# Decay rows of two chunked scans: from a select matmul to a masked fill and an accumulating DMA

## The chip, the cores and the metric

The kernel runs on one core of a Trainium2 chip. The metric is the device time of one execution in microseconds (us); lower is better.

## What is computed

The reference is one step of a two-layer diffusion backbone over 640 tokens (128 of context, 512 of a latent grid) with a model width of 1024. Each layer has a normalised and modulated input, one wide input projection, three bidirectional recurrent mixers side by side (an SSD scan with 16 heads in 4 groups, an HGRN2 scan with 4 heads, an mLSTM scan with 4 heads), gated merging, an output projection, and a gated feed-forward block. Only the decay matrices of two of the scans matter here. In the SSD scan, with `la` the cumulative log decay inside a chunk:

```python
la = jnp.cumsum(dtc * a[:, None], axis=-1)
diff = jnp.where(causal, la[..., :, None] - la[..., None, :], 0.0)
seg = jnp.exp(diff) * causal * dtc[..., None, :]
```

The mLSTM scan has the same form: an exponential of a term of the row (time) plus a term of the column (source), zero where the mask forbids. The backward direction has the opposite triangle.

## The kernel before

The tokens are cut into five chunks of 128 (`NCH`), the first of which is the context. Activations are kept transposed, with features on the 128 partitions. Weights arrive as 512 KB tiles on the SyncE DMA queue (`weight_load`, called `wr` in the trace; three buffers), are split by ScalarE and VectorE into a rounded part and a remainder (`wh`, `wl`; four buffers each), and each tile of a projection is three matmuls of 320 columns per half and per block of 128 rows (`project`, `accumulate`, line 495).

TensorE's order is written out by hand: `drive` runs a scan as a generator and, at every `yield n`, runs n steps of the projections that still wait ("bulk"; one step is six matmuls of 320 columns). So a scan's own matmuls are strewn among projection matmuls. The order on ScalarE, VectorE, SyncE and GpSimd is chosen at build time by a planner, which goes by the order of the program and by when it takes operands and buffers to be free; at run time each queue is strictly in order. GpSimd does nothing but issue DMAs (`load`, line 138); SyncE issues those of `stream` (line 141). Most intermediate tiles come from one pool of 35 buffers of 128x656 (`ut`).

How the decay matrices come about, for one scan and one direction d:

- `store_rows` (line 798) transposes the cumulative decays of all heads and chunks into rows, splits each into a rounded part `rwh` and a remainder `rwl`, sets the remainder at the edge position to -1e30, and stores both in DRAM (`rows_s`, `rows_m`).
- `new_rows` (line 945) makes `NROW` = 2 buffers `rb` for each direction, filled by ScalarE with the additive mask (0 or -1e30), four copies side by side.
- `fetch_rows` (line 954) overwrites two partitions of such a buffer, those at the edge of the triangle, with the two parts of the rows, by a DMA of 2 to 4 KB on GpSimd's queue.
- `row_bank` (line 961) is the matmul that does both jobs: its stationary operand `rsel` is an identity in which the two partitions of the rows have ones in every column. The product in PSUM is the mask plus the row, on all 128 partitions.
- ScalarE takes the exponential from PSUM, with the column's term as its bias, into a tile `E` (SSD, line 1175; four heads of one chunk, four instructions of 128x128) or `mA` (mLSTM, line 1452; one head, chunk by chunk).

```python
rows = [row_bank(d, flats[c][d], 4) for d in range(2)]
fetch(c + NROW)
for d, pt in enumerate(rows):
    e = ut("E")
```

In `ssd_scan`, `stage_a(c)` holds these lines; `stage_b(c)` (the matmuls `py` that use `E`) comes two chunks later (`LAGB`), and the first two fetches are made at the first of the four state updates (after the copy `cx`). In `mlstm_scan` the rows of a head are fetched at its start, and are used after the four state updates, in two groups of three and two chunks. There are 4 SSD scans and 4 mLSTM scans per layer, 8 and 8 in the program.

## Time and profile before

| | |
|---|---|
| median of 3 runs | 2811.21 us (2811.20 to 2813.16) |
| the profiled execution, its own time | 2809.44 us |
| its span, first to last instruction | 2807.7 us |
| TensorE busy in the span | 2765.0 us (98%) |
| share of TensorE in the chain that ended last | 94% |
| matmuls of `row_bank` (line 963) | 112 |
| moved by DMA | 347.97 MB, 16 engines 37.4% busy on average |

The profile lists each engine's busy time, the waits with what ended them, and a timeline. A busy TensorE here is one that always has a next matmul at hand; consecutive matmuls overlap, so what one costs is the distance from its start to the start of the next, not its duration.

### The profile page before, as it was taken

The numbers are of one execution on the slowest core, as the hardware profiler recorded it, in microseconds if no ns is written. First come the engines' busy times: TensorE is split into PE (matmuls) and PEld (weight loads), VectorE is DVE, ScalarE is ACT, GpSimd is POOL, SyncE is SP. The second block draws the span as 40 slices with busy tenths as digits, with TensorE's granted clock in tenths as the row PEclk, the third lists the DMA queues.
The fourth block names the chain that finished last, engine by engine and source line by source line (L and its number), as shares of the span: only waits on it lengthen the run. The fifth ranks groups of instructions, "written<-read, shape, count | busy, mean of one in ns | idle before, by whom it ended". The sixth has DMA issues, their size and how long they took to land.

```text
span 2807.7 us, 48854 instructions
## 1 busy us (share of the span) xinstructions
PE 2765.0 (98%) x19374; PEld 2714.7 (97%) x19374; DVE 1902.0 (68%) x3862; ACT 1227.6 (44%) x2453; POOL 265.0 (9%) x499
## 2 busy tenths in 40 slices
PE   7999999999999999999999999999999999999998
PEld 6999999999999999999999999999999999999998
DVE  6566668777655586867776665878775556747475
ACT  5534434445542363343455444344455225425243
POOL 0111100001031100000001111000111201000000
PEclk9999999999999999999999999999999999999999
DMA  8222223333374314344522222333333732333433
GB/s 322 90 93 80 89 85 111 128 117 117 125 256 148 108 63 155 126 132 156 175 98 86 83 91 94 106 114 128 121 112 119 258 106 96 100 128 103 130 108 100
DMA packets 102579, 347.97 MB, mean 124 GB/s; under 512 B 18784, under 2 KB 22080, under 8 KB 102224
## 3 DMA queue, kind: packets, MB, share of 16 engines
q1 hardware_dynamic: 70704, 243.34, 26.2%
q0 software_dynamic: 31648, 101.52, 10.7%
q8 instruction: 153, 2.51, 0.4%
q14 instruction: 74, 0.61, 0.1%
HBM read 290.37 MB, written 54.42 MB: 123 GB/s over the span
## 4 chain that ended last, share of the span: by engine, by line
PE 94%; DVE 3%; ACT 2%; DMA 1%; issue 1%; SPq 0%; ACTq 0%; DVEq 0%
PE ga L423 17%; PE ab L495 15%; PE bg L495 12%; PE br L495 8%; PE sz L495 4%; PE hfp L495 4%; PE xT L495 4%; PE hl L1328 2%; PE ga L495 2%; PE hgp L495 2%; PE hqp L495 2%; PE mkp L495 2%; PE BT L495 2%; PE CT L495 2%; PE mop L495 1%; PE mqp L495 1%
## 5 line engine op out<-in xcount | busy, mean ns | idle before, releaser
L412 ACT ACTIVATE wh<-wr 128x1024 fp32r<-128x1024 f32 (+3 forms) x354 | 352.7, 1000 | 545.1 <-PE br L495 144.3
L413 DVE TENSOR_TENSOR wl<-wr,wh 128x1024 fp32r<-128x1024 f32 (+3 forms) x354 | 406.1, 1148 | 198.8 <-ACT wh L412 194.6
L423 PE MATMUL ga<-hb,wh 128*128 128x320 f32 x912 | 201.4, 308 | 0.0
L1588 DVE SCALAR_TENSOR_TENSOR x<-ab,hg,x 128x128 f32<-128x128 f32 (+2 forms) x192 | 73.2, 433 | 170.1 <-PE ab L495 170.1
L423 PE MATMUL ga<-hth,wl 128*128 128x320 f32 x608 | 187.7, 309 | 0.0
L423 PE MATMUL ga<-htl,wh 128*128 128x320 f32 x608 | 187.4, 308 | 0.0
L423 PE MATMUL ga<-hth,wh 128*128 128x320 f32 x608 | 187.4, 308 | 0.0
L495 PE MATMUL bg<-hh,wh 128*128 128x320 f32 x768 | 186.5, 324 | 0.0
L495 PE MATMUL bg<-hl,wh 128*128 128x320 f32 x768 | 174.8, 309 | 0.0
L495 PE MATMUL bg<-hh,wl 128*128 128x320 f32 x768 | 174.6, 308 | 0.0
L495 PE MATMUL ab<-uh,wh 128*128 128x320 f32 x704 | 164.5, 309 | 0.0
L495 PE MATMUL ab<-ul,wh 128*128 128x320 f32 x704 | 164.1, 309 | 0.0
L495 PE MATMUL ab<-uh,wl 128*128 128x320 f32 x704 | 164.0, 308 | 0.0
L423 PEld LDWEIGHTS ga<-hb,wh 128*128 128x128 f32 x912 | 152.4, 188 | 0.0
L423 PE MATMUL ga<-hb,wl 128*128 128x320 f32 x456 | 140.7, 308 | 0.0
L495 PEld LDWEIGHTS bg<-hh,wh 128*128 128x128 f32 x768 | 126.5, 189 | 2.4 <-issue 0.8
L495 PEld LDWEIGHTS bg<-hl,wh 128*128 128x128 f32 x768 | 128.4, 188 | 0.0
L495 PEld LDWEIGHTS bg<-hh,wl 128*128 128x128 f32 x768 | 128.4, 188 | 0.0
L495 PEld LDWEIGHTS ab<-ul,wh 128*128 128x128 f32 x704 | 118.8, 188 | 0.2
L495 PEld LDWEIGHTS ab<-uh,wh 128*128 128x128 f32 x704 | 118.6, 188 | 0.2
L495 PEld LDWEIGHTS ab<-uh,wl 128*128 128x128 f32 x704 | 118.7, 188 | 0.0
L423 PEld LDWEIGHTS ga<-hth,wh 128*128 128x128 f32 x608 | 114.3, 188 | 0.0
(505 smaller groups left out, 7542.0 us busy)
## 6 DMA issues: line engine op xcount, KB each, us to landing
wr<-w_in SPq DMA_DIRECT2D x152, 512.0 KB, 3.4
wr<-w_gu SPq DMA_DIRECT2D x88, 512.0 KB, 3.8
wa<-w_ada SPq DMA_DIRECT2D x84, 512.0 KB, 3.6
x<-xd POOLq DMA_DIRECT2D x64, 320.0 KB, 3.6
wr<-w_down SPq DMA_DIRECT2D x32, 512.0 KB, 3.8
sp<-bgt POOLq DMA_DIRECT2D x48, 320.0 KB, 3.4
bgr<-sp POOLq DMA_DIRECT2D x48, 320.0 KB, 4.8
xd<-x POOLq DMA_DIRECT2D x40, 320.0 KB, 2.5
```

The lines of the kernel that those rows point to most:

```text
L412: act.activation(out=hi[:, :n], in_=raw[:, :n], func=AF.Copy)
L413: dve.tensor_tensor(out=lo[:, :n], in0=raw[:, :n], in1=hi[:, :n].bitcast(F32), op=ALU.subtract)
L423: pe.matmul(bank_[:, :HALF], a_[:, sl], b_, start=first and j == m == 0, stop=j == n - 1 and m == 2, skip_group_check=True,)
L495: pe.matmul(out[hf][:, :HALF], wt_[:, sl], b_, start=m == k == 0, stop=m == 2 and k == n - 1)
L1328: pe.matmul(pt[:, (c - c0) * P : (c - c0 + 1) * P], kk[:, sl], halves_of(QK[:, 0, sl], 3 * T, L, P // (2 * L)), start=True, stop=True,)
L1588: dve.scalar_tensor_tensor(out=x_[:, lo:hi], in0=pt[:, lo - hf * HALF : hi - hf * HALF], scalar=gate[:, 2 * f + j : 2 * f + j + 1], in1=x_ ...
```

## The change

The matmul, its stationary operand and its mask buffers are removed. The rows are stored once, in full float32. For each `E` or `mA` tile a DMA on SyncE's queue first copies the mask into it (128 partitions, four or five times the same 128 floats), and then a DMA on GpSimd's queue adds the rows to it, read from DRAM for every partition anew. The exponential runs in place, from SBUF. An SSD scan fetches as many chunks ahead as before, but into `E` itself; an mLSTM scan fills both whole `mA` tiles at its start.

```diff
-        rows_s = dr.tile([4, NCH, SH, P], F32R, name=nm("rows_s"), tag="rows_s")
-        rows_m = dr.tile([2, 2, NCH, MH, P], F32R, name=nm("rows_m"), tag="rows_m")
+        rows_s = dr.tile([2, NCH, SH, P], F32, name=nm("rows_s"), tag="rows_s")
+        rows_m = dr.tile([2, NCH, MH, P], F32, name=nm("rows_m"), tag="rows_m")
...
-        def store_rows(src, n, d, dst_of):
+        def store_rows(src, n, d, dst):
             pt = bank("rows")
             pe.transpose(pt[:n, :P], src, ident)
-            hi = ut("rwh", F32R)
-            lo = ut("rwl", F32R)
-            act.activation(out=hi[:n, :P], in_=pt[:n, :P], func=AF.Copy)
-            dve.tensor_tensor(out=lo[:n, :P], in0=pt[:n, :P], in1=hi[:n, :P].bitcast(F32), op=ALU.subtract)
-            act.activation(out=lo[:n, EDGE[d] : EDGE[d] + 1], in_=cc[:n, C_MASKF, 0:1], func=AF.Copy, scale=0.0, bias=NEG)
-            load(dst_of(0), hi[:n, :P])
-            load(dst_of(1), lo[:n, :P])
+            row = ut("rw")
+            act.activation(out=row[:n, :P], in_=pt[:n, :P], func=AF.Copy)
+            act.activation(out=row[:n, EDGE[d] : EDGE[d] + 1], in_=cc[:n, C_MASKF, 0:1], func=AF.Copy, scale=0.0, bias=NEG)
+            load(dst, row[:n, :P])
...
-        def new_rows():
...
-        def fetch_rows(d, src, n):
...
-        def row_bank(d, flat, n):
-            pt = bank("row")
-            pe.matmul(pt[:, : n * P], rsel[:, d, :], flat[:, : n * P], start=True, stop=True)
-            return pt
+        def masked_rows(d, out, src, n):
+            v = out.rearrange("p (n t) -> p n t", t=P)
+            stream(v, cc[:, C_MASKF + d, :].unsqueeze(1).to_broadcast([P, n, P]))
+            nc.gpsimd.dma_start(out=v, in_=src.unsqueeze(0).to_broadcast([P, n, P]), accum_op=ALU.add)
+            return out
...
-                    flats[c] = [fetch_rows(d, rows_s[2 * d : 2 * d + 2, c, hsl, :], 4) for d in range(2)]
+                    flats[c] = [masked_rows(d, ut("E")[:, :512], rows_s[d, c, hsl, :], 4) for d in range(2)]
...
-                    if g == 0:
-                        new_rows()
...
-                E = []
-                rows = [row_bank(d, flats[c][d], 4) for d in range(2)]
+                E = flats.pop(c)
                 fetch(c + NROW)
-                for d, pt in enumerate(rows):
-                    e = ut("E")
+                for d, e in enumerate(E):
                     for j in range(4):
                         act.activation(
-                            out=e[:, j * P : (j + 1) * P], in_=pt[:, j * P : (j + 1) * P], func=AF.Exp,
+                            out=e[:, j * P : (j + 1) * P], in_=e[:, j * P : (j + 1) * P], func=AF.Exp,
...
-            if hd == 0:
-                new_rows()
-            flats = [[fetch_rows(d, rows_m[:, d, c0:c1, hd, :], c1 - c0) for d in range(2)] for c0, c1 in groups]
+            A = [masked_rows(d, ut("mA")[:, :T], rows_m[d, :, hd, :], NCH) for d in range(2)]
...
-            A = [ut("mA") for _ in range(2)]
...
-                    pt = row_bank(d, flats[c0 > 0][d], n)
                     for c in range(c0, c1):
                         sl = slice(c * P, (c + 1) * P)
-                        act.activation(out=A[d][:, sl], in_=pt[:, (c - c0) * P : (c - c0 + 1) * P], func=AF.Exp, bias=ptr("ma", d, c))
+                        act.activation(out=A[d][:, sl], in_=A[d][:, sl], func=AF.Exp, bias=ptr("ma", d, c))
```

The input `rsel`, its load and its rounding copy go too.

## Rows read from the trace of the kernel before

**Rows 1.** The page, busy us, share of the span and instructions.

```profile
PE 2765.0 (98%) x19374; PEld 2714.7 (97%) x19374; DVE 1902.0 (68%) x3862; ACT 1227.6 (44%) x2453; POOL 265.0 (9%) x499
```

**Rows 2.** Waits of PE in 90 to 420 and 620 to 780: us, times, longest.

```profile
PE hl L1328 <- ACT hk L1316: 0.2, 1, 0.2
...
PE htr L1252 <- DVE mo__1073_6954 L1246: 1.5, 1, 1.5
PE mup L1429 <- DVE vw L1426: 0.3, 1, 0.3
```

**Rows 3.** Windows: length, busy PE, PEld, DVE, ACT, POOL, clock, DMA share, GB/s.

```profile
90.00:400.00 310.00, 310.00 (x2152) 296.48 (x2151) 193.06 (x407) 141.15 (x344) 38.86 (x75) 1.00 0.26 85
198.00:238.00 40.00, 40.00 (x269) 37.49 (x268) 29.47 (x60) 22.01 (x57) 5.52 (x11) 1.00 0.22 76
620.00:770.00 150.00, 148.10 (x1099) 147.03 (x1098) 105.08 (x302) 80.50 (x210) 17.97 (x32) 1.00 0.39 126
```

**Rows 4.** Line 963: count, ns min/median/max, first and last start, forms.

```profile
L963 PE MATMUL row<-rb,rsel x112: 277/392/425, 125.1 to 2135.7; 128*128 128x512 f32 x80, 128*128 128x384 f32 x16, 128*128 128x256 f32 x16
```

**Rows 5.** Timeline of PE, an SSD scan and an mLSTM scan: start, us, instruction.

```profile
208.29 0.45 PE L495 MATMUL xT<-hh,wl 128*128 128x320 f32 x2
208.58 0.63 PE L963 MATMUL row<-rb,rsel 128*128 128x512 f32 x2
209.05 0.45 PE L495 MATMUL xT<-hh,wh 128*128 128x320 f32 x2
...
641.93 0.60 PE L963 MATMUL row<-rb,rsel 128*128 128x384 f32 x2
642.37 0.46 PE L495 MATMUL mkp<-hh,wh 128*128 128x320 f32 x2
...
645.36 0.48 PE L963 MATMUL row<-rb,rsel 128*128 128x256 f32 x2
645.68 0.46 PE L495 MATMUL mkp<-hh,wh 128*128 128x320 f32 x2
```

**Rows 6.** Timeline, second SSD scan: ACT's copy and exponentials, PE's users of E.

```profile
197.44 0.60 ACT L1149 ACTIVATE cx<-sup 128x512 f32<-128x512 f32 x1 [2.31 <-issue]
209.02 2.18 ACT L1175 ACTIVATE E<-row,gsb 128x128 f32<-128x128 f32 x8 [0.85 <-PE row L963]
...
217.08 0.66 PE L1192 MATMUL py<-E,sA 128*64 128x128 f32 x8
...
241.80 0.66 PE L1192 MATMUL py<-E,sA 128*64 128x128 f32 x8
```

**Rows 7.** Groups of instructions: count, busy us, mean ns, idle before and releaser.

```profile
L413 DVE TENSOR_TENSOR wl<-wr,wh 128x1024 fp32r<-128x1024 f32 x294 | 359.1, 1222 | 193.5 <-ACT wh L412 191.4
...
L138 POOL DMA_DIRECT2D rb<-rows_s x80 | 40.0, 504 | 159.1 <-PE row L963 158.1 <-ACT rb L949 0.8
L1180 DVE TENSOR_TENSOR E<-E,E 128x512 f32<-128x512 f32 x40 | 27.7, 692 | 47.5 <-ACT E L1175 47.4
L1181 DVE TENSOR_TENSOR E<-E,cbs 128x512 f32<-128x512 f32 x40 | 27.5, 687 | 0.7
```

**Rows 8.** DMA queue in 99 to 102 (four stores of 512 B rows): packets, MB, share.

```profile
q0 software_dynamic: 384, 0.16, 35.2%
```

**Rows 9.** A window in which full weight tiles arrive; columns as in rows 3.

```profile
627.00:627.50 0.50, 0.50 (x6) 0.50 (x5) 0.30 (x2) 0.16 (x1) 0.00 (x0) 1.00 1.00 410
```

**Rows 10.** DMA issues: count, KB each, median us to landing.

```profile
hs<-s_ssm POOLq DMA_DIRECT2D x8, 256.0 KB, 4.4
o_ssm<-cx POOLq DMA_DIRECT2D x8, 256.0 KB, 2.3
```

**Rows 11.** Timelines of SPq (second SSD scan) and POOL (first mLSTM scan).

```profile
195.49 47.90 SPq L141 DMA_DIRECT2D wr<-w_in  x6
...
633.33 1.74 POOL L138 DMA_DIRECT2D rb<-rows_m  x3 [8.26 <-ACT rb L949]
```

**Rows 12.** SPq's DMA instructions of weight loads: ns min/median/max.

```profile
L141 SPq DMA_DIRECT2D wr<-w_in x152: 327/328/381, 9.7 to 2137.1; - x152
```

More of the change, by code (lines that the diff above doesn't have):

```diff
@@ L178, in backbone @@
     lmask = cst.tile([P, len(LEVELS), P], U8, name="lmask")
-    rsel = cst.tile([P, 2, P], F32R, name="rsel")
     normf = cst.tile([P, KT], F32, name="normf")
@@ L844, in gates @@
             for d in range(2):
-                store_rows(la[:, d].rearrange("p c h -> p (c h)"), 80, d, lambda w, d=d: rows_s[2 * d + w].rearrange("c h t -> (c h) t"))
+                store_rows(la[:, d].rearrange("p c h -> p (c h)"), 80, d, rows_s[d].rearrange("c h t -> (c h) t"))
             dtv = dt.rearrange("p c (d h) -> p d c h", d=2)
@@ L915, in mgates @@
             for d in range(2):
-                store_rows(nbm[:, d].rearrange("p c h -> p (c h)"), 20, d, lambda w, d=d: rows_m[w, d].rearrange("c h t -> (c h) t"))
+                store_rows(nbm[:, d].rearrange("p c h -> p (c h)"), 20, d, rows_m[d].rearrange("c h t -> (c h) t"))
             mp = g4("gmp", 4)
@@ L941, in mgates @@
             yield 1
-        rowbufs = [[], []]
-        def new_rows():
-            for d in range(2):
-                rowbufs[d] = [ut("rb", F32R) for _ in range(NROW)]
-                for b_ in rowbufs[d]:
-                    act.activation(
-                        out=b_[:, :512].rearrange("p (r f) -> p r f", f=P),
-                        in_=cc[:, C_MASKF + d, :].unsqueeze(1).to_broadcast([P, 4, P]), func=AF.Copy,
-                    )
-        def fetch_rows(d, src, n):
-            b_ = rowbufs[d].pop(0)
-            rowbufs[d].append(b_)
-            r0 = (0, P - 2)[d]
-            load(b_[r0 : r0 + 2, : n * P].rearrange("p (h t) -> p h t", t=P), src)
-            return b_
-        def row_bank(d, flat, n):
-            pt = bank("row")
-            pe.matmul(pt[:, : n * P], rsel[:, d, :], flat[:, : n * P], start=True, stop=True)
-            return pt
+        def masked_rows(d, out, src, n):
[3 more added lines that the diff above has]
+            return out
         def head_rstd(ssq):
@@ L1168, in stage_a @@
                 sl = slice(c * P, (c + 1) * P)
-                E = []
-                rows = [row_bank(d, flats[c][d], 4) for d in range(2)]
+                E = flats.pop(c)
                 fetch(c + NROW)
-                for d, pt in enumerate(rows):
-                    e = ut("E")
+                for d, e in enumerate(E):
                     for j in range(4):
                         act.activation(
-                            out=e[:, j * P : (j + 1) * P], in_=pt[:, j * P : (j + 1) * P], func=AF.Exp,
+                            out=e[:, j * P : (j + 1) * P], in_=e[:, j * P : (j + 1) * P], func=AF.Exp,
                             bias=gv["sb"][:, d, c, 4 * g + j : 4 * g + j + 1],
                         )
-                    E.append(e)
                 dve.tensor_tensor(out=E[0][:, :512], in0=E[0][:, :512], in1=E[1][:, :512], op=ALU.add)
@@ L1775, in late_constants @@
         dve.tensor_scalar(out=fbi, in0=hcum, scalar1=0.5, scalar2=0.5, op0=ALU.mult, op1=ALU.add)
-        sel = ut("sel")[:, : 2 * P].rearrange("p (d f) -> p d f", d=2)
-        load(sel, a["rsel"])
-        act.activation(out=rsel, in_=sel, func=AF.Copy)
         for m in range(2):
@@ L1966 @@
               np.where(le > 0, 0.0, NEG).astype(f32), np.where(le.T > 0, 0.0, NEG).astype(f32)]
-    sels = []
-    for d in range(2):
-        sel = np.eye(P, dtype=f32)
-        sel[[(0, 1), (P - 2, P - 1)][d], :] = 1.0
-        sels.append(sel)
-    arr["rsel"] = np.stack(sels, 1)
     arr["consts"] = np.stack(consts, 1)
```

## The prediction

> **What bounds the kernel.** I read the page first: TensorE is busy for 98% of the span, VectorE for 68%, ScalarE for 44% [rows 1]. An average hides stages, so I then read the waits of TensorE in the stages that hold the change. In the four SSD scans of the first layer it waited 0.2 us in 330 us, in the mLSTM scans 1.8 us in 160 us [rows 2]. The windows say the same: 310.00 busy of 310.00 in the SSD stage, 148.10 of 150.00 in the mLSTM stage, the clock at 1.00 throughout, which is the higher of its two levels, 2.4 GHz [rows 3]. So in exactly these stages TensorE runs without a gap, in an order fixed by hand, and every matmul taken out shortens the path by its own distance to the next start, as long as nothing that it now waits for comes later. ScalarE, VectorE, GpSimd and the DMA engines (share 0.26 and 0.39) have room [rows 3].
>
> **What is removed.** 112 matmuls: 80 of 512 columns, 16 of 384, 16 of 256 [rows 4]. They stand in pairs. From the start of a pair to the start of what follows: 209.05 - 208.58 = 0.47 us with 512 columns, 642.37 - 641.93 = 0.44 with 384, 645.68 - 645.36 = 0.32 with 256 [rows 5]. The sum is 40 x 0.47 + 8 x 0.44 + 8 x 0.32 = 18.8 + 3.5 + 2.6 = 24.9 us. A second way: a pair of 320-column matmuls takes 208.58 - 208.29 = 0.29 us [rows 5], 0.46 ns a column; 80 x 512 + 16 x 384 + 16 x 256 = 51,200 columns make 23.5 us. I take 24. Off the path, and so worth nothing by themselves, go the mask copies on ScalarE, the subtraction and half of the row stores, the load of the select matrix, and 112 small issues on GpSimd of 0.5 us [rows 7]. The cover is TensorE's own 100%; were it gone, ScalarE at 44% would still have room.
>
> **What is added.** 96 pairs of DMAs: 80 of 256 KB (4 heads) and 16 of 320 KB (5 chunks).
>
> SyncE: 96 issues of about 0.33 us [rows 12], ten in a scan, 3.3 us in a stretch in which that queue has six weight loads in 48 us [rows 11]. A fill that waits for its buffer holds the weight loads queued behind it. The weights are three raw and four split tiles ahead, and a tile of a projection is 48 matmuls of 0.147, 7 us of TensorE; a hold under some 20 us reaches nobody. I cost it at nothing; without that cover it would be 3.3 us a scan, 26 us over eight.
>
> GpSimd: 96 accumulating issues in the place of 112 small ones. I cost an issue at the 0.5 us that it has now [rows 7]; the trace has no accumulating one. Each waits for its fill to land, and behind it in the queue stand spills of finished tiles and loads of states. The same queue waits today for the select matmul, 158 us in all [rows 7], without harm to TensorE.
>
> DMA engines: the trace shows neither a copy inside SBUF nor an accumulation, so I bound both. A fill moves 512 pieces of 512 B, 32 an engine. Four stores of 80 rows of 512 B took 35.2% of 16 engines for 3 us [rows 8], 16.9 engine-us over 320 rows, 53 ns each: 1.7 us a fill. The other end is bulk speed, 410 GB/s [rows 9]: 0.64 us. An accumulation must read the tile and the row and write the sum: between 0.64 us (bulk, one read) and 2 x 1.7 = 3.4 us (two reads in pieces of 512 B). A pair then costs 1.3 to 5.1 us of all 16 engines. The rows of one chunk lie together in DRAM, 2 KB for four heads, so I put the accumulation near two bulk reads, 1.3 us, and the fill, whose source really is in 512 B pieces, at about 1.2, the middle of its bounds: 2.5 us a pair.
>
> What can a scan afford? In the second SSD scan the first fetch follows the copy at 197.4, and the last user of an `E` starts at 241.8 [rows 6]. Before that user come 2.2 us of exponentials [rows 6] and 1.4 us of VectorE [rows 7]. That leaves until 238, 40 us for ten pairs, of which other transfers take 0.22 [rows 3]: 31 us, 3.1 us a pair. At 2.5 the transfers fit, with a sixth to spare; at 3.1 they stop fitting. That is the point on which the sign turns.
>
> Latency: issue 0.3, fill landed 2.3 to 4.4 us after (the 256 KB transfers of [rows 10]), issue 0.5, sum landed 2.3 to 4.4: 5.4 to 9.6 us. The first chunk has 209.0 - 198 = 11 us from the fetch to today's exponentials [rows 6], later chunks two chunk steps and no longer a matmul to wait for, since nothing of TensorE stands before the exponential now. In the first mLSTM scan the fetch is at 633.3 [rows 11] and the exponentials follow the matmul at 641.9 [rows 5], 8.6 us, with two pairs of 320 KB: I charge 1 us there in each layer, 2 us. The lower bound of this term is nothing, or a gain of the 1.8 us that TensorE waits in that stage now.
>
> ScalarE: 400 exponentials read SBUF in place of PSUM. They come at 2.18 / 8 = 0.27 us apart [rows 6]; even 0.1 us more each is 40 us on an engine that is 46 to 54% busy in these stages [rows 3]. Nothing. The new wait matters more: an exponential now waits on ScalarE for a landing, and queued behind it are evictions of projections and weight splits. TensorE needs an evicted bank again one whole projection tile later, 7 us, but a copy inside a scan's head is awaited two steps later, 1.8 us. That is the second rival.
>
> **A rule against the change.** The add needs two operands, so I let the upper bound read twice; no row of this trace can show that. The Trainium skill ("Collectives: The Full Stack", section "The bandwidth ceiling: the fold count and why AG ≠ RS ≠ AR") says that an add in the DMA datapath is slower for its two source reads, which share one ring. By it one read is excluded, a pair in pieces of 512 B would be 1.7 + 3.4 = 5.1 us, and the first rival's time would be the sum; with one read it would be 3.4, which nearly fits.
>
> **The sum.** The profiled execution took 2809.4 us, 1.7 more than its span, and stands 1.8 us below the median. 2809.4 - 24 + 2 = 2787.4; against the median, 2811.2 - 24 + 2 = 2789 us.
>
> **Rivals.**
> First, slower: the DMA engines can't supply the scans. Place: the ten pairs of an SSD scan; point: 3.1 us a pair to be late at all, and 3.1 + 24 / 80 = 3.4 to eat the gain. For it: the upper bound of 5.1, and that all 128 partitions read the same 2 KB of DRAM, which nothing in the trace prices. Against it: the share is only 0.22 now, and the four buffers `rb` that were held between scans are free, so the first chunks can be filled while the scan before still runs. At 4.1 us, halfway to the bound, the last `E` is 10 us late in each of eight scans: 2811 - 24 + 80 = 2867; at the bound 2947.
>
> Second, the gain is given back in ScalarE's queue: one hold of about 2.5 us that reaches TensorE in each of the eight SSD scans, at a transposing copy or at the first exponentials. 8 x 2.5 = 20 us; 2811 - 24 + 20 = 2807, which the clock can't tell from no change (0.2%, 5.6 us, is about what a measurement of this kernel can). For it: 9.6 us of latency at the slow end against 11. Against it: the first exponentials are done at 211.2 and VectorE's 1.4 us later, and their user starts at 217.1 [rows 6], 4.5 us of slack.
>
> Third, GpSimd's issue of an accumulation is held by VectorE's work, which is 74% busy there [rows 3]. The longest common instruction on VectorE takes 1.2 us (the weight remainder, 1222 ns) [rows 7]; one such delay reaching TensorE in each of 16 scans gives 19 us, 2806. Against it: the small issues average 504 ns beside the same VectorE [rows 7].
> The Trainium skill ("SBUF — State Buffer", section "SBUF: two separate sides") describes such a block for DMAs issued from GpSimd, 620 ns becoming about 3100; the trace's 504 ns doesn't agree with it here.
>
> **How the numbers follow.** Forecast 0.56; first rival 0.27; second 0.13; third 0.04. Faster by over 0.2% (below 2805.6) is the forecast, 0.56. The second, in the most of its cases, and the third fall within: 0.14. The first, and 0.03 of the second where holds are longer, are slower: 0.30. The range begins at 2811.2 - 24.9 - 1.8 = 2784, the greatest removal with the old waits gone, and reaches to 2860, where the first rival has less than half of its chance beyond. The forecast's own range is 2784 to 2800.
>
> **What would show it.** Right: no line 963; TensorE's waits in the SSD stages still under a few us; busy time of TensorE lower by more than the 24 us (overlapping durations); fill and accumulation together under 3.1 us of engine time; DMA share in 198 to 238 about 0.22 + 25 / 40 = 0.8. The forecast is wrong if TensorE waits at `py` for VectorE or ScalarE and those for a DMA into `E` (first rival), if waits of 2 us stand at the copies of a scan's head (second), or if GpSimd's issues grow past 1 us (third).

## The result and the profile after

The changed kernel takes 2898.39 us (median of 6 runs, 2893.39 to 2903.92), the kernel before 2811.36 (6 runs beside it): a ratio of 1.0307, 95% interval 1.0296 to 1.0318. It is slower by 87 us where 22 us less was forecast.

The page of the changed kernel: engines, the two large DMA queues, the chain that ended last, the new DMA issues (count, KB each, median us to landing), the exponentials of the SSD scans.

```profile
PE 2782.6 (96%) x19262; PEld 2721.4 (94%) x19262; DVE 1896.1 (66%) x3854; ACT 1231.7 (43%) x2436; POOL 297.2 (10%) x474
...
q1 hardware_dynamic: 123440, 269.56, 28.8%
q0 software_dynamic: 48368, 126.98, 16.2%
...
PE 73%; DMA 10%; DVE 6%; issue 6%; ACT 3%; POOL 1%; SPq 1%; POOLq 0%; ACTq 0%; DVEq 0%
...
L1150 ACT ACTIVATE E<-E,gsb 128x128 f32<-128x128 f32 x320 | 103.1, 391 | 122.1 <-DMA E<-rows_s 121.9
...
E<-cc SPq DMA_DIRECT2D x80, 256.0 KB, 6.5
E<-rows_s POOLq DMA_DIRECT2D x80, 256.0 KB, 7.4
```

The 112 matmuls are gone: 19262 in place of 19374 [rows 1]. Yet TensorE is busy for longer, 2782.6 us against 2765.0, and fills only 96% of a longer span. The chain has left TensorE for 27% of the span, in place of 6%, and 10% of the span are DMA's. The new transfers land in 6.5 and 7.4 us; the two 256 KB transfers that the prediction took as a measure landed in 4.4 and 2.3 [rows 10].

Where the time went is read by stage. I call "SSD stage" the time from the first `sup` matmul to the first `hd` (the four SSD scans of a layer), "mLSTM stage" that from the first `mup` to the last `mpn`; both come from the instructions of those tiles, and every other stage between them is as long as before to within 2 us. All figures in this table are us of the profiled execution.

| kernel | to the first `sup` | SSD, layers 1, 2 | mLSTM, layers 1, 2 |
|---|---|---|---|
| before | 112.0 | 296.5, 296.1 | 133.9, 133.2 |
| after | 117.9 | 321.3, 322.9 | 150.6, 145.4 |
| SSD scans alone changed | 117.3 | 328.9, 317.6 | 133.8, 133.4 |
| mLSTM scans alone changed | 114.6 | 296.4, 296.6 | 142.6, 147.4 |
| no rows at all | 115.7 | 287.1, 287.0 | 131.5, 130.9 |
| fills alone | 114.5 | 287.1, 287.3 | 136.1, 133.4 |
| mask copied by ScalarE | 115.3 | 297.4, 296.4 | 156.9, 161.9 |
| spreading DMA, VectorE mask | 115.8 | 289.7, 291.2 | 152.9, 147.7 |
| four chunks ahead | 115.2 | 317.9, 318.9 | 148.1, 148.3 |
| unread pairs beside the old way | 113.0 | 328.4, 333.8 | 135.4, 133.7 |
| mask from DRAM | 114.7 | 322.2, 320.8 | 150.4, 146.4 |
| mLSTM fills a head earlier | 116.2 | 321.2, 331.7 | 150.1, 150.3 |
| SSD: VectorE mask | 114.6 | 290.4, 293.8 | 133.8, 133.3 |
| mLSTM: placed late | 114.2 | 296.4, 296.6 | 144.8, 142.6 |
| SSD: fetched early, placed late | 114.6 | 314.0, 314.0 | 133.9, 133.5 |
| SSD: placed late | 112.9 | 298.0, 299.1 | 133.7, 133.4 |
| SSD: fills on GpSimd's queue | 117.4 | 319.5, 319.5 | 133.7, 133.3 |
| whole change, order repaired | 114.0 | 296.9, 300.6 | 140.0, 138.1 |
| SSD: VectorE mask, placed late | 114.8 | 287.1, 286.8 | 133.8, 133.2 |

From before to after: 24.8 + 26.8 in the SSD stages, 16.7 + 12.2 in the mLSTM stages, 5.9 at the start, 86.4 of the 86.2 us by which the span grew. (The start differs by up to 6 us among all these kernels, those without the change's transfers too; I did not follow it.)

Windows of the changed kernel, the first layer's two stages and a stretch within; columns as in [rows 3].

```profile
117.90:439.20 321.30, 300.65 (x2013) 284.51 (x2012) 185.85 (x387) 136.15 (x317) 50.37 (x68) 0.96 0.55 144
666.50:817.10 150.60, 136.32 (x964) 132.96 (x964) 96.11 (x285) 67.95 (x182) 16.96 (x18) 0.97 0.51 141
...
119.00:144.00 25.00, 25.00 (x172) 23.95 (x170) 13.89 (x28) 12.54 (x32) 7.53 (x9) 1.00 0.93 217
...
148.00:152.00 4.00, 1.60 (x11) 1.33 (x10) 3.12 (x7) 3.24 (x7) 1.73 (x2) 1.00 0.37 78
152.00:156.00 4.00, 2.19 (x10) 1.89 (x12) 2.84 (x8) 1.71 (x6) 0.00 (x0) 0.69 0.79 195
...
144.00:169.00 25.00, 20.30 (x120) 18.31 (x116) 18.70 (x42) 12.49 (x29) 1.73 (x2) 0.86 0.42 110
```

TensorE now stands still for 321.30 - 300.65 = 20.65 us of the SSD stage, where it had not a gap [rows 3], and its clock is 0.96. The two windows of 4 us show the pair of losses: TensorE idles for 2.4 us of four, and in the next four its granted clock is 0.69, part of it at the lower of the two levels, 1.2 GHz. The DMA engines are at 0.93 in the first 25 us of the chunk loop, with TensorE still unharmed there; in the next 25 us it stands still for 4.7 us (25.00 - 20.30).

Waits of TensorE in the changed kernel (us in all, times, longest):

```profile
PE sz L494 <- DVE cu L999: 14.0, 4, 4.5
PE pi L1175 <- DVE y L1176: 12.6, 6, 4.0
...
PE mpn L1434 <- DVE mA L1426: 9.2, 3, 3.6
PE BT L494 <- DVE cu L999: 7.3, 2, 3.8
PE mup L1401 <- DVE vw L1398: 7.2, 8, 2.0
```

And of ScalarE and VectorE, in the same kernel:

```profile
ACT E L1150 <- DMA E<-rows_s: 121.9, 72, 7.7
...
ACT mA L1422 <- DMA mA<-rows_m: 69.6, 16, 9.3
...
DVE E L1154 <- ACT E L1150: 85.6, 30, 7.6
```

TensorE waits little for the products with `E` themselves. It waits at `sz` and `BT`, projection matmuls whose PSUM banks are held by `cu`, the convolution of another projection, and at `pi` for `y`. Those are VectorE's, and VectorE stands in turn at the sums of the two directions' `E`, which wait for ScalarE's exponentials (85.6 us, against 47.4 before [rows 7]), and ScalarE waits 121.9 us in 72 waits for accumulations to land. That reading names a path, not yet what makes it: the transfers' number, their latency, or the order. The experiments below part these.

### The profile page after: what moved, and what is told of

It reads as the page before. It is cut to its first block, busy times and chain, and to the rows that moved or that the text cites. A ratio compares the mean times of both kernels' runs of the same rounds, so it can differ in the third digit from the quotient of the medians.

```text
span 2893.9 us, 48625 instructions
## 1 busy us (share of the span) xinstructions
PE 2782.6 (96%) x19262; PEld 2721.4 (94%) x19262; DVE 1896.1 (66%) x3854; ACT 1231.7 (43%) x2436; POOL 297.2 (10%) x474
## 3 DMA queue, kind: packets, MB, share of 16 engines
q1 hardware_dynamic: 123440, 269.56, 28.8%
q0 software_dynamic: 48368, 126.98, 16.2%
## 4 chain that ended last, share of the span: by engine, by line
PE 73%; DMA 10%; DVE 6%; issue 6%; ACT 3%; POOL 1%; SPq 1%; POOLq 0%; ACTq 0%; DVEq 0%
PE ga L422 16%; PE ab L494 14%; PE bg L494 8%; PE br L494 8%; PE hfp L494 3%; DMA E<-cc 3%; DMA E<-rows_s 3%; PE hl L1302 2%; DMA mA<-rows_m 2%; PE sz L494 2%; PE ga L494 2%; PE xT L494 2%; PE hgp L494 1%; PE hqp L494 1%; DVE wl L412 1%
## 5 line engine op out<-in xcount | busy, mean ns | idle before, releaser
L1150 ACT ACTIVATE E<-E,gsb 128x128 f32<-128x128 f32 x320 | 103.1, 391 | 122.1 <-DMA E<-rows_s 121.9
```

The source lines that it names most:

```text
L1150: act.activation(out=e[:, j * P : (j + 1) * P], in_=e[:, j * P : (j + 1) * P], func=AF.Exp, bias=gv["sb"][:, d, c, 4 * g + j : 4 * g + j + 1],
```

## Experiments

**The two halves.** One kernel changes only the SSD scans, one only the mLSTM scans.

```diff
# SSD half; the mLSTM half likewise
-flats[c] = [fetch_rows(d, rows_s[2 * d : 2 * d + 2, c, hsl, :], 4) for d in range(2)]
+flats[c] = [masked_rows(d, ut("E")[:, :512], rows_s[d, c, hsl, :], 4) for d in range(2)]
```

> The change in the SSD scans alone; the mLSTM scans keep the matmul. Theory (tiles E come late, since two DMAs in a row stand between a buffer and its exponential; the stage of the first SSD scans grew by some 31 us in the first layer, start included, and by 27 in the second): 2811 + 31 + 27 = about 2865. Rival (the mLSTM scans' fills of 640 pieces do most of the harm, by holding the queues): under 2830.

Measured 2873.44 us, 1.0217 (1.0202 to 1.0233).

> The change in the mLSTM scans alone; the SSD scans keep the matmul. Theory: 2811 + 16 + 12 = about 2835 to 2840, so that the two parts add up to the whole. Rival: the parts don't add (one needs the other's load on the DMA engines), and this one alone is within 5 us of before.

Measured 2840.44 us, 1.0104 (1.0086 to 1.0122). Both halves are slower, and they add up: 61.3 + 28.3 = 89.6 us, against 87. Both came out near what was expected of them.

**What the matmuls are worth.** The exponentials read the constant mask.

```diff
-    stream(v, cc[:, C_MASKF + d, :].unsqueeze(1).to_broadcast([P, n, P]))
-    nc.gpsimd.dma_start(out=v, in_=src.unsqueeze(0).to_broadcast([P, n, P]), accum_op=ALU.add)
...
-out=e[:, j * P : (j + 1) * P], in_=e[:, j * P : (j + 1) * P], func=AF.Exp,
+out=e[:, j * P : (j + 1) * P], in_=cc[:, C_MASKF + d, :], func=AF.Exp,
```

> Leaves the rows out altogether: no matmul, no fill, no accumulation; the exponentials read the mask from its constant tile, without a bias. Theory (the matmuls were on the path, at 0.46 ns a column): 2811 - 24 = about 2787. Rival (the matmuls were worth nothing, or the planner's new order by itself costs time): 2805 or more.

Measured 2791.55 us, 0.9925 (0.9910 to 0.9940). The four stages are shorter by 9.4, 9.1, 2.4 and 2.3 us: 23.2, where the prediction took 24. I take this time, and these stages, as the floor for the change. TensorE in this kernel, by the page:

```profile
PE 2748.2 (98%) x19262; PEld 2700.2 (97%) x19262; DVE 1898.4 (68%) x3854; ACT 1191.7 (43%) x2436; POOL 201.9 (7%) x378
```

And in its first SSD stage, a window with columns as in [rows 3]:

```profile
115.70:402.80 287.10, 287.10 (x2012) 275.41 (x2012) 187.13 (x387) 119.14 (x317) 15.15 (x28) 1.00 0.26 88
```

The same 19262 matmuls took 2782.6 us in the changed kernel, 34.4 more, and the mean granted clock of the execution is 0.985 in place of 0.996: I put that part of its loss down to the lower clock. The other 68.8 us of the 103.2 between the two spans are idle TensorE.

**Which transfer.** Fills alone, and accumulations onto a mask that ScalarE copies.

```diff
# fills alone
-    nc.gpsimd.dma_start(out=v, in_=src.unsqueeze(0).to_broadcast([P, n, P]), accum_op=ALU.add)
# mask by ScalarE
-    stream(v, cc[:, C_MASKF + d, :].unsqueeze(1).to_broadcast([P, n, P]))
+    act.activation(out=v, in_=cc[:, C_MASKF + d, :].unsqueeze(1).to_broadcast([P, n, P]), func=AF.Copy)
```

> As the changed kernel without the accumulating DMAs: the exponentials wait for the fills alone (the rows are left out, and the bias). Theory (the accumulation is the larger half: in the run with ScalarE's fills the SSD stages came back to 297 us from 322, and without any DMA they take 287): the fill alone costs 5 us or less a layer, 2791 to 2803. Rival (the fill's landing of 6.5 us is as harmful as the sum's of 7.4): 2830 or more.

Measured 2798.17 us, 0.9946 (0.9926 to 0.9966; two runs). The fills land in 4.9 us here:

```profile
E<-cc SPq DMA_DIRECT2D x80, 256.0 KB, 4.9
```

> As the changed kernel, but the mask is copied into the tiles by ScalarE (0.62 us a tile) in place of the DMA on SyncE's queue. Theory (two landings in a row, 6.5 and 7.4 us, and DMA engines that are full in bursts): one landing goes and 1 us of 2.8 a pair, so well over half of the loss goes: 2800 to 2850. Rival (the accumulation alone is too slow, or GpSimd's queue is): 2880 or more.

Measured 2866.24 us, 1.0187 (1.0172 to 1.0203): a miss. The SSD stages do come back to the length of before, 297.4 and 296.4, but the mLSTM stages grow to 156.9 and 161.9. So in the SSD scans neither transfer alone does the harm, 0 and 10 us above the floor; together they cost 34 and 36. (Each of these edits also makes the planner set the queues anew; how much that matters only the later runs bring out.) And the mLSTM scans suffer from something that isn't the fill at all. Its trace says where, in a wait of TensorE that the changed kernel hardly has (7.2 us there):

```profile
PE mup L1401 <- DVE vw L1398: 35.5, 10, 5.6
...
692.55 0.17 DVE L1423 COPY mA<-gmed 128x3 f32<-128x3 f32 x1 [6.67 <-ACT mA L1422]
692.63 0.28 DVE L1398 TENSOR_SCALAR vw<-val,gmwk 128x129 f32<-128x129 f32 x1
```

`vw` is a small product that needs nothing of `mA`; it is queued on VectorE behind a copy into `mA`, which waited 6.67 us for ScalarE's exponentials.

**No accumulation.** A plain DMA spreads the rows, VectorE adds the mask.

```diff
-    stream(v, cc[:, C_MASKF + d, :].unsqueeze(1).to_broadcast([P, n, P]))
-    nc.gpsimd.dma_start(out=v, in_=src.unsqueeze(0).to_broadcast([P, n, P]), accum_op=ALU.add)
+    stream(v, src.unsqueeze(0).to_broadcast([P, n, P]))
+    dve.tensor_tensor(out=v, in0=v, in1=cc[:, C_MASKF + d, :].unsqueeze(1).to_broadcast([P, n, P]), op=ALU.add)
```

> As the changed kernel, but a plain DMA on SyncE's queue brings the rows to all partitions, and VectorE adds the mask (0.69 us a tile). Theory (two landings in a row and an accumulation of 1.75 us of all engines): one plain landing, no GpSimd, so the loss goes and the matmuls' gain shows, less some of VectorE's 66 us of adds: 2790 to 2815. Rival (any transfer of 256 KB a tile in this chain is late, or 128 partitions reading one row of DRAM is what is slow): 2850 or more.

Measured 2833.52 us, 1.0068 (1.0051 to 1.0085): a miss, and again by the mLSTM stages (152.9, 147.7; TensorE waits 26.4 us at `mup` for `vw`). The SSD stages, 289.7 and 291.2, are shorter than before, for the first time with the rows in them. The same with the mLSTM scans left as they were:

> The kernel before with the SSD scans alone changed, in another way: a plain DMA on SyncE's queue spreads the 2 KB of rows over the partitions of E, one VectorE instruction adds the mask, and the exponentials run in place; the mLSTM scans keep select matmul and mask buffers. No accumulation, one landing in place of two. Theory: the loss of the SSD scans is that of the second transfer, since the same edit beside changed mLSTM scans gave stages of 290 and 291 us against 296 before; so stages of 289 to 292, mLSTM stages as before (133 to 136), and 2798 us (2793 to 2804), faster than both. Rival: the order of the other engines around it, which the planner sets anew, takes the gain back: 2806 to 2820.

Measured 2805.39 us, 0.9973 (0.9961 to 0.9984; 6 runs): faster than both kernels, by less than expected.

**More chunks ahead, and the load without the waits.** `NROW = 4` in the changed kernel; and the old way with a pair of transfers beside every fetch, into tiles that nobody reads.

```diff
-NROW = 2
+NROW = 4
# the other kernel, from the kernel before; the same in mlstm_scan
+for d in range(2):
+    masked_rows(d, rows_s[2 * d, c, hsl, :].bitcast(F32), 4)
 flats[c] = [fetch_rows(d, rows_s[2 * d : 2 * d + 2, c, hsl, :], 4) for d in range(2)]
```

> As the changed kernel, with four chunks fetched ahead in an SSD scan in place of two. Theory (latency: a pair takes some 14 us in a row, and is asked for 11 us ahead): the SSD stages fall from 322 to below 305 us, the mLSTM stages stay, 2850 to 2870. Rival (throughput: the engines can't move ten pairs in a scan): 2885 or more, the stages still above 315.

Measured 2888.04 us, 1.0266 (1.0250 to 1.0281), SSD stages 317.9 and 318.9: more tiles asked for at the same point bring 3 to 4 us a stage, as its rival had it, and not the 17 that the theory wanted.

> The kernel before, with the 96 pairs of DMAs added at the same places of the program into tiles that nothing reads. Theory (the harm is in the wait of the exponentials, not in the load on queues and engines): 2811 to 2822. Rival (the load itself delays weights, spills and states): 2840 or more.

Measured 2883.12 us, 1.0249 (1.0234 to 1.0264): a miss. The SSD stages are as long as with the change, though no exponential waits for a pair. This looks like a proof that the load itself is to blame, but the trace shows a detour. TensorE's largest wait:

```profile
PE row L971 <- DMA rb<-rows_s: 30.2, 11, 6.6
```

The rows of the select matmul are loaded on GpSimd's queue, and that queue now holds accumulations that wait for their fills. So the run shows what such a queue does to its neighbours, and can't tell load from order.

**Size of the pieces.** The mask lies in DRAM at full width, so that a fill is 128 pieces of 2 KB in place of 512 of 512 B.

```diff
-    stream(v, cc[:, C_MASKF + d, :].unsqueeze(1).to_broadcast([P, n, P]))
+    stream(out, wmd[d, :, : n * P])
```

> The changed kernel with one thing different: the mask lies in DRAM at full width (written once at the start), so that a fill is 128 pieces of 2 KB (2.5 KB in the mLSTM scans) in place of 512 or 640 pieces of 512 B. Bytes, issues, order and waits stay. Theory 'pieces' (fills of 512 B pieces that alternate with the accumulations on the 16 engines are what makes the SSD scans late: fills alone cost nothing there, accumulations alone 10 us over no rows, both 34): the fill lands in under 5 us (6.5 in the changed kernel), the two SSD stages fall from 321 and 323 us to 297 to 307, and the time to about 2850 (2835 to 2865). Rival 'bytes' (what saturates is the bytes and the accumulation's second read, whatever the pieces): the SSD stages stay at 314 or more and the time at 2880 to 2900. The mLSTM stages stay near 150 and 145 by both.

Measured 2886.88 us, 1.0259 (1.0241 to 1.0278), SSD stages 322.2 and 320.8; the fills land in 6.7 us. The pieces are not it.

**The mLSTM fills a head earlier.**

```diff
+if n == 3 and hd < MH - 1:
+    mA_next[hd + 1] = fill(hd + 1)
```

> The changed kernel with one thing different: an mLSTM scan issues the fill and accumulation for the next head behind its own fourth state update, so that three heads of four in each layer have their tiles some 20 us earlier; two more tiles are held meanwhile. Theory 'landing' (in the mLSTM scans the exponentials stand in ScalarE's queue ahead of work that TensorE waits for, and are held by an accumulation that lands 7 to 9 us after a 1.5 us issue): the mLSTM stages fall from 150.6 and 145.4 us to 133 to 139, ScalarE's wait for the accumulation into mA from 70 us to under 25, and the time to about 2876 (2868 to 2884). Rival 'traffic' (the issue on GpSimd's queue and the transfers themselves disturb the stage, wherever they stand): the stages stay at 143 or more, the time at 2890 or more. The SSD stages stay near 321 and 323.

Measured 2908.69 us, 1.0340 (1.0324 to 1.0355), mLSTM stages 150.1 and 150.3: no help. What became of the early transfers is the turn of the study. Timelines of GpSimd's and ScalarE's `mA` instructions in the first head:

```profile
673.98 4.58 POOL L942 DMA_DIRECT2D mA<-rows_m  x3 [7.37 <-DMA mA<-cc]
...
681.13 1.57 ACT L1427 ACTIVATE mA<-mA,gma 128x128 f32<-128x128 f32 x5 [10.04 <-DMA mA<-rows_m]
683.01 1.28 ACT L1427 ACTIVATE mA<-mA,gma 128x128 f32<-128x128 f32 x4 [0.30 <-DMA mA<-rows_m]
684.86 0.99 ACT L1427 ACTIVATE mA<-mA,gma 128x128 f32<-128x128 f32 x3 [0.57 <-DMA mA<-rows_m]
686.96 0.97 ACT L1427 ACTIVATE mA<-mA,gma 128x128 f32<-128x128 f32 x3
```

The accumulations of the second head are issued with the first head's last one, as intended. But the second head's ten exponentials (683.01 to 686.96) have moved forward with them, a whole head. The planner puts an exponential into ScalarE's queue as soon as it takes the tile to be there; before, the select matmul in TensorE's fixed order had held it back. So here an earlier transfer only brought its exponentials forward, and they waited for it as before.

**Place alone, SSD scans.** The exponentials' bias is copied by a small VectorE instruction that also reads the bank of the fourth state update, times zero. The transfers stay as the change has them; the planner can no longer place the exponentials ahead of that point. It plans all four queues anew around this.

```diff
+if n == 3:
+    sbp = small("sbp", 40).rearrange("p (d c h) -> p d c h", d=2, h=4)
+    dve.scalar_tensor_tensor(
+        out=sbp, in0=pt[:, :40].rearrange("p (d c h) -> p d c h", d=2, h=4), scalar=0.0,
+        in1=gv["sb"][:, :, :, hsl], op0=ALU.mult, op1=ALU.add,
+    )
...
-bias=gv["sb"][:, d, c, 4 * g + j : 4 * g + j + 1],
+bias=sbp[:, d, c, j : j + 1],
```

> The control of the one above: the kernel before with the SSD scans alone changed and the bias copied behind the fourth state update, fetches where the change has them. Theory 'crowding': no help, SSD stages of 312 to 332, time of 2850 to 2885. Rival 'place' (what hurts in the SSD scans is that exponentials stand early in ScalarE's queue): stages of 305 or less, time of 2840 or less.

Measured 2820.00 us, 1.0024 (1.0015 to 1.0034; 10 runs), SSD stages 298.0 and 299.1. "Crowding", which I held for the likelier, falls as the main cause: the same 80 pairs cost 53 us less in another order (2873.44 to 2820.00), and the engines are no emptier. Two windows of this kernel, columns as in [rows 3]:

```profile
115.00:140.00 25.00, 25.00 (x170) 23.86 (x170) 13.51 (x29) 11.26 (x31) 9.19 (x11) 1.00 0.98 226
140.00:165.00 25.00, 22.63 (x157) 20.70 (x156) 23.45 (x54) 13.30 (x29) 0.57 (x1) 1.00 0.37 103
```

In the second window TensorE stands still for 2.4 us and keeps its clock; in the changed kernel's (144 to 169) it was 4.7 us and a clock of 0.86. Of the 53 us some 49 lie in the SSD stages (328.9 + 317.6 - 298.0 - 299.1); the start is 4 us shorter.

The two orders side by side. First the changed kernel's ScalarE in the first chunk loop (its copy `cx` ended at 119.55):

```profile
127.45 1.28 ACT L1150 ACTIVATE E<-E,gsb 128x128 f32<-128x128 f32 x4 [1.45 <-DMA E<-rows_s]
130.16 1.28 ACT L1150 ACTIVATE E<-E,gsb 128x128 f32<-128x128 f32 x4 [1.44 <-DMA E<-rows_s]
131.71 1.28 ACT L1150 ACTIVATE E<-E,gsb 128x128 f32<-128x128 f32 x4 [0.27 <-DMA E<-rows_s]
132.90 0.72 ACT L1004 ACTIVATE xT<-cu 128x640 f32<-128x640 f32 x1
134.80 1.28 ACT L1150 ACTIVATE E<-E,gsb 128x128 f32<-128x128 f32 x4 [1.18 <-DMA E<-rows_s]
135.99 1.04 ACT L411 ACTIVATE wh<-wr 128x1024 fp32r<-128x1024 f32 x1
```

Its SyncE in the same stretch:

```profile
126.26 0.34 SPq L141 DMA_DIRECT2D wr<-w_in  x1
126.64 5.31 SPq L141 DMA_DIRECT2D E<-cc  x4
138.70 0.33 SPq L141 DMA_DIRECT2D wr<-w_in  x1
139.13 1.50 SPq L141 DMA_DIRECT2D E<-cc  x2
```

And ScalarE of the kernel placed late (`cx` ended at 114.58, 5 us earlier):

```profile
124.01 0.74 ACT L1039 ACTIVATE xT<-cu 128x640 f32<-128x640 f32 x1 [2.99 <-issue]
126.27 4.80 ACT L1191 ACTIVATE E<-E,sbp 128x128 f32<-128x128 f32 x16 [1.52 <-DVE sbp L1177]
130.98 1.11 ACT L1021 ACTIVATE cu<-xT,pv 128x320 f32<-128x320 f32 x2
```

Its SyncE:

```profile
121.67 8.83 SPq L141 DMA_DIRECT2D E<-cc  x6
```

In the changed kernel four tiles are taken one by one, each as it lands, 1.5 to 3 us apart, and the activation `xT` stands between them; VectorE's last addition into the states, queued behind the second half of `xT`, starts 14.9 us after `cx` ended (134.40) in place of 10.1 (124.70). Placed late, the same sixteen exponentials run in one go, 4.80 us, each tile being there when its turn comes, and `xT`, now ahead of them, starts 9.4 us after `cx` ended in place of 13.4. Up to there the transfers went out alike: GpSimd issued the first four accumulations 3.0 and 5.2 us after `cx` ended in the changed kernel (122.53, 124.71, two each), 3.0 and 5.3 us after it in the other (117.55, 119.87). So in this stretch it is the order that differs, not the transfers. SyncE shows a loop: in the changed kernel the last fills stand behind a weight load that goes out at 138.70, once ScalarE and VectorE have split an earlier tile (ScalarE's `wh`, 135.99), which stood behind exponentials, which waited for accumulations. In the other plan the last six fills went out from 121.67, ahead of any such load. What was not parted is which of the reordered queues carries how much of the 53 us.

**Fetched early as well.** The first four chunks are asked for at the scan's start.

```diff
+for c in range(NROW):
+    fetch(c)
 for j in range(2):
     transpose_into(xT[j], lambda c0, c1, j=j: xtv[:, c0:c1, j * P : (j + 1) * P])
```

> The kernel before with the SSD scans alone changed, as in the first run, with the first four chunks' fills and accumulations asked for at the scan's start, some 20 us ahead of the first state update, and the exponentials' bias copied behind the fourth state update so that they don't move forward with them. The same number of transfers, over about twice the time. Theory 'crowding' (ten pairs and the weights fill the 16 engines for the 30 us in which they are asked for): the SSD stages fall from 329 and 318 us to 290 to 303, and the time from 2873 to 2822 (2805 to 2838). Rival 'interference' (the transfers disturb as much wherever they stand, by their bytes or by holding the queues): stages of 312 or more, time of 2850 or more.

Measured 2851.07 us, 1.0132 (1.0116 to 1.0147), stages of 314.0: worse than late placing alone, and a miss. The exponentials no longer wait for a landing, something else does, VectorE's `xw`, a small product for the state updates:

```profile
DVE xw L1147 <- DMA sp<-bgt: 78.3, 7, 11.9
```

The buffer that `xw` needs is freed by a spill, a DMA on GpSimd's queue, where accumulations wait for their fills. The wait has only changed its place.

**Fills on GpSimd's queue**, away from the weights.

```diff
-    stream(v, cc[:, C_MASKF + d, :].unsqueeze(1).to_broadcast([P, n, P]))
+    nc.gpsimd.dma_start(out=v, in_=cc[:, C_MASKF + d, :].unsqueeze(1).to_broadcast([P, n, P]))
```

> The kernel before with the SSD scans alone changed, and the fills issued by GpSimd instead of SyncE, so that they neither stand behind weight loads on one queue nor hold them. Theory 'crowding': the engines are as full and GpSimd now has twenty issues of 0.9 us with a wait in each second one; stages of 312 or more, time of 2850 or more. Rival 'shared queue' (fills land in 8 to 10 us in place of 4.9 because 512 KB of weights stand ahead of them on SyncE's queue): stages of 295 to 308, time of 2815 to 2840.

Measured 2861.41 us, 1.0169 (1.0153 to 1.0184), stages of 319.5: sharing a queue with the weights is not the main cause either.

**Place alone, mLSTM scans.** The same device behind the score matmuls.

```diff
+dve.scalar_tensor_tensor(
+    out=mb_.rearrange("p (d c) -> p d c", d=2), in0=sc[:, : 2 * n].rearrange("p (d c) -> p d c", d=2), scalar=0.0,
+    in1=gv["ma"][:, :, c0:c1, hd], op0=ALU.mult, op1=ALU.add,
+)
```

> The kernel before with the mLSTM scans alone changed, as in the second run, and one thing more: the bias of the exponentials is copied by a small VectorE instruction that also reads the score bank (times zero), so that the planner can place them only behind the score matmuls, where they stood while they waited for the select matmul. The transfers and their landing stay. Theory 'place' (the exponentials stand too early in ScalarE's queue, since the planner counts the tile as ready, and hold what TensorE waits for): the mLSTM stages fall from 142.6 and 147.4 us to 131 to 136, and the time from 2840 to 2818 (2808 to 2824). Rival 'landing' (the sum lands too late for the products wherever the exponentials stand): the stages stay at 141 or more, the time at 2836 or more.

Measured 2833.61 us, 1.0073 (1.0058 to 1.0088), stages of 144.8 and 142.6: a miss. The fills of a head are still issued only at its start, and the sums land too late for the new place: TensorE's largest wait in the stages is 10.5 us for the products with `mA`. The earlier transfer and the late place together, with the SSD scans' late placing, in the whole change:

> The whole change, with the order repaired in three places: the SSD exponentials' bias copied behind the fourth state update, the mLSTM exponentials' bias copied behind the score matmuls, and the fill and accumulation of the next mLSTM head issued behind the fourth state update of the one before. Transfers as in the changed kernel. Theory 'place and landing': the SSD stages are 297 to 300 us as in the run before; the mLSTM stages, in which three heads of four now have their sums early and their exponentials late, fall from 150.6 and 145.4 to 133 to 139 (the first head's second fill still comes late); the time is 2818 (2810 to 2828) in place of 2898. Rival 'issue' (the 1.5 us issues and the late buffers disturb the mLSTM stages anyhow): mLSTM stages of 142 or more, time of 2830 or more. Were the select matmuls' 23 us to come back in full, it would be about 2790; neither theory expects that.

Measured 2829.03 us, 1.0060 (1.0046 to 1.0073): 69 us better than the change, at the edge of what "place and landing" expected, with mLSTM stages of 140.0 and 138.1. In the first of them TensorE has one large wait left, the first head's second tile, which this edit didn't make earlier:

```profile
656.26 0.77 PE L1450 MATMUL mpn<-val,mA 128*128 128x129 f32 x2 [5.72 <-DVE mA L1442]
```

So in the mLSTM scans neither an earlier transfer (150.1, 150.3) nor a later place (144.8, 142.6) did much alone, and both together give back 18 of the 33.6 us that the changed kernel's two stages stand above the floor. Some 16 us (140.0 + 138.1 - 131.5 - 130.9) remain, of which that wait is the only large piece I can name in the first layer.

**A version that beats both.** The plain spreading DMA and VectorE's mask in the SSD scans alone, with the mask addition placed behind the fourth state update.

```diff
+zc = small("zc", 1)
+dve.tensor_scalar(out=zc, in0=pt[:, 0:1], scalar1=0.0, scalar2=None, op0=ALU.mult)
...
+dve.scalar_tensor_tensor(
+    out=v, in0=v, scalar=zc, in1=cc[:, C_MASKF + d, :].unsqueeze(1).to_broadcast([P, 4, P]),
+    op0=ALU.add, op1=ALU.add,
+)
```

> The SSD scans alone changed as in the third run of the batch before last (plain spreading DMA, mask added by VectorE, mLSTM scans as in the kernel before), with the mask addition placed behind the fourth state update by a zero column that it reads, so that neither it nor the exponentials can stand early. Theory 'place': the SSD stages fall from 290.4 and 293.8 us to 287 to 290, and the time from 2805 to 2799 (2796 to 2804). Rival (the mask addition's own time on VectorE, ten of some 0.7 us a scan, is what is left): stages and time as they were, 2803 to 2810.

Measured 2792.92 us, 0.9930 (0.9917 to 0.9944; 5 runs): 19 us faster than the kernel before, beyond what was expected. Its first SSD stage (columns as in [rows 3]) is the floor of the kernel without rows, 287.10 us without a gap:

```profile
114.80:401.90 287.10, 287.10 (x2013) 275.44 (x2012) 212.01 (x433) 133.82 (x317) 16.08 (x30) 1.00 0.43 124
```

VectorE is 25 us busier in the stage, and that costs nothing. In the SSD scans, then, the select matmul can be taken out at no cost to TensorE, with one landing and a late place; with two landings and a late place (298.0, 299.1) 11 to 12 us a stage are lost again. In the mLSTM scans VectorE's mask ran only in the planner's own order (152.9, 147.7); with a late place it is untried.

## Why the prediction was wrong

**The sum.** Predicted: -24 for the matmuls, nothing in the SSD scans, +2 in the mLSTM scans. Measured, by stages against the floor: -23.2, +70.1 in the SSD scans (34.2 + 35.9), +33.6 in the mLSTM scans (19.1 + 14.5), and 5.9 at the start, not followed: 86.4 us.

**What bounds the kernel, and the removal: right.** 23.2 us by stages, 24 predicted; the floor is 2791.55 us, and 2811.2 - 24 is 2787. Only the sign that it named was not met: TensorE's busy time is lower by 16.8 us there (2765.0 - 2748.2), not by more than 24.

**DMA engines: about right in size, wrong as a criterion.** The two large queues of the kernel before, and the hardware queue of the kernel with VectorE's mask placed late (packets, MB, share):

```profile
q1 hardware_dynamic: 70704, 243.34, 26.2%
q0 software_dynamic: 31648, 101.52, 10.7%
...
q1 hardware_dynamic: 82224, 264.32, 30.2%
```

From before to after the hardware queue grew from 26.2% of 2807.7 to 28.8% of 2893.9 us, 98 us over 96 fills, 1.02 each; the software queue from 10.7% to 16.2%, 168 us, net of the small loads that went, 1.75 an accumulation. A pair is 2.77 us of all 16 engines, predicted 2.5, below the turning point of 3.1. The share was 0.93 over the first 25 us, predicted 0.8. By this step the scans should have been supplied, and with late placing they were more nearly, at a share of 0.98: 7.15 us of gaps in the first SSD stage (298.00 - 290.85) in place of 20.65. A supply that suffices on average says nothing about the order in which the tiles come and who stands behind each.

The prediction weighed a rule of the Trainium skill here ("Collectives: The Full Stack", section "The bandwidth ceiling: the fold count and why AG ≠ RS ≠ AR"), that an add in the DMA datapath pays for two source reads. An accumulation took 1.75 us against 1.02 for a fill of as many bytes in smaller pieces, which is dearer, as the rule has it; with 2.77 for the pair the time it warned of (5.1) did not come. The nearer measure says that the add is the smaller part: a plain DMA that spreads the same rows over the same 80 tiles took 107 us more than the queue had before (30.2% of 2791.6 us against 735.6), 1.34 each, and 1.55 in the run that spreads the mLSTM rows as well (31.2% of 2835.0 us). These are estimates, good to some 0.15 us: without any rows the same queue took 26.8% of 2790.7 us, 12 more than before. The two kinds of DMA also go through different queues. So spreading one row over all 128 partitions, which nothing in the trace of the kernel before prices, takes some 1.2 to 1.6 us of the 16 engines without an add.

**Latency: wrong.** "fill landed 2.3 to 4.4 us after" and "sum landed 2.3 to 4.4" came from two plain transfers of the kernel before. They landed in 6.5 and 7.4 us, beside each other and the weights, 4.9 for a fill without accumulations; one of the two that served as the measure, `o_ssm`, itself went from 2.3 to 5.2 us in the changed kernel. With the issues that is some 15 us in place of 5.4 to 9.6, more than the 11 us that the first chunk had.

**SyncE: mis-sized, and looked at from one side.** An issue of a fill took 0.70 us at the median and 6.7 at the longest, in place of the 0.33 of a weight load [rows 12]:

```profile
L141 SPq DMA_DIRECT2D E<-cc x80: 593/704/6657, 117.5 to 1809.8; - x80
```

The prediction asked whether fills hold weight loads. Hardly: the one wait of TensorE that the profile puts down to ScalarE's weight split is 1.7 us. The timelines above show the reverse, fills behind a weight load, though that isn't the main cause by itself either: with the fills on GpSimd's queue the stages were 319.5.

**ScalarE: the step that failed.** The forecast set the SSD scans at nothing, since the tile would be there (5.4 to 9.6 us) within the 11 us before the old exponential. The second rival, "one hold of about 2.5 us that reaches TensorE in each of the eight SSD scans", had the mechanism and a chance of 0.13, and it was mis-sized: ScalarE waited 121.9 us, 15 us a scan, in 72 holds, and the SSD stages lost 70.1 us against the floor, 8.8 a scan in place of 2.5. The prediction asked whether the tile would be there when the old exponential ran. The exponential didn't stay there: the matmul that was removed had also been what held it back in the planned order, and nothing in the text counted that. Late placing gives back 53 of the SSD half's 61 us (2873.44 to 2820.00). That shows the order as the main cause in the SSD scans; which queue's order carries it stays open. It cost this much only where two landings stand in a row: in the planner's own order the stages were 287.1 and 287.3 with fills alone, 297.4 and 296.4 with the mask copied by ScalarE, and with the plain DMA late placing was worth 3 and 7 us a stage. Nor did the sum hold a term for the clock, which made 34 of the 103 us above the floor.

**First rival: its number, not its mechanism.** 2867 us was the nearest of the forecasts, which is luck: its place, the supply, is not where most of the time was lost.

**mLSTM: mis-sized.** 2 us predicted beside the removal, 33.6 measured against the floor (28.9 against the kernel before). The issue took 1.5 us in place of 0.5, the landing 7.3, and the first head's second fill came 9 us after its first (655.7 and 664.7). GpSimd's `mA` instructions in the changed kernel, ns min/median/max, first and last start, and their landing:

```profile
L942 POOL DMA_DIRECT2D mA<-rows_m x16: 1490/1528/2185, 661.3 to 2215.9; - x16
...
DMA to landing us min/median/max: 6.0/7.3/9.2
```

**Third rival: not borne out.** Issues of the SSD accumulations have a median of 0.92 us and a longest of 1.92, with VectorE 66% busy; the Trainium skill's case ("SBUF — State Buffer", section "SBUF: two separate sides"), about 3.1 us, was not seen. The sign that the prediction named, issues past 1 us, did come in the mLSTM scans, at 1.53; but the shortest there is 1.49, so it reads as the price of those issues and not as a hold. What did matter on that queue, in two of the runs, is what the prediction named and gave no cost, the loads and spills behind a waiting accumulation: 30.2 us of TensorE's waits in the run with unread pairs, 78.3 us of VectorE's in the one fetched early.

**Exponentials from SBUF: right.** Sixteen take 4.80 us, 0.30 each, 0.27 before [rows 6].

## What to carry to other kernels

A matmul in a fixed order is also a gate: before it is taken out, ask what will stand where on the in-order queues once nothing holds it back, and put the gate back (here a zero read from the right bank) if the planner counts a DMA's tile as ready too early. Count a chain of two DMAs by their landings in the crowd, not alone, and put an upper bound on every engine that waits for them, since all that is queued behind waits too. One plain DMA and an addition on an engine with room beat a fill and an accumulating DMA in the SSD scans here.

## What was not expected of the hardware

- An accumulating DMA of 256 or 320 KB took 1.75 us of the 16 engines on average, and those of 256 KB landed in 7.4 us; GpSimd's issue took 0.92 us for 128 rows of 2 KB and 1.53 us for 640 pieces of 512 B. The same rows spread without the add took an estimated 1.2 to 1.6 us.
- Fills of 2 KB pieces from DRAM did no better than 512 B pieces out of SBUF: 6.7 and 6.5 us to landing, the hardware queue at 28.2% and 28.8%.
- DMA engines at a mean share of 0.93 and of 0.98 for 25 us left TensorE without a gap in these 25 us. In the next 25 us it stood still for 4.7 us in the order with the lower share and for 2.4 us in the other.
